# A second and third copy of the values in HBM, and attention units in mirrored order, on one Trainium2 core

## The chip, the cores and the metric

The kernel runs on one NeuronCore of a Trainium2 chip. Its engines run their own instruction queues and meet at semaphores: PE (TensorE, matrix products; the trace shows its weight loads apart as PEld), DVE (VectorE), ACT (ScalarE), POOL (GpSimd) and SP (SyncE, which here only issues DMAs). The metric is the device time of one execution in microseconds (us). A change of this kernel's time is told from no change at about 0.5%, some 14 us.

## The reference

One layer of a hybrid decoder, for a prompt of 2048 tokens and 64 sample tokens. The part that the change touches is the prompt's attention: 8 heads of 64 elements, and for each head three patterns of window and dilation, whose results are merged by their softmax denominators. Cut to that:

```
PATTERNS = ((128, 1), (512, 4), (2048, 16))          # window, dilation; n = window // dilation = 128

def dilated_prompt(q, k, v, window, dil):            # query t reads keys t - j*dil, j = 0..128
    qb, kb, vb = to_blocks(q), to_blocks(k), to_blocks(v)   # residue mod dil, blocks of 128
    kk, vv = with_prev(kb), with_prev(vb)                   # a block and the one before it
    s = jnp.einsum('brhcie,brhcje->brhcij', qb, kk) * (E ** -0.5)
    s = jnp.where(mask, s, NEG)                             # band, and no block before the first
    lse = jax.nn.logsumexp(s, axis=-1)
    p = jnp.exp(s - lse[..., None])
    return jnp.einsum('brhcij,brhcje->brhcie', p, vv), lse  # back in token order

def combine_patterns(results):
    w = jax.nn.softmax(lses, axis=0)
    return jnp.sum(w[..., None] * outs, axis=0)
```

Before it stand the projections of q, k, v and of a gated linear attention; behind it the output projection and a convolutional feed-forward network. Everything is float32; the large products are made of two fp32r parts each (high and low).

## The kernel before

**Stages.** By the trace, the projections of the linear attention run from 0 to about 480 us; the projections of q, k and v (`sweep_a`, one call per chunk of 512 tokens, in the order 3, 0, 1, 2), woven with the sample tokens' attention, from 480 to 780 us; the prompt's attention (`attention`) from 780 to 1090 us; the output projection and the feed-forward network from 1090 us to the end.

**Values.** `sweep_a` makes the values in tiles `vs` of 128 tokens by 256 elements (4 heads), 8 tiles per chunk. DVE copies each out of PSUM (L63), and one DMA of 128 KB stores it in the output `o_vp` (L453): on SP's queue for the chunks 3, 0 and 1, on POOL's for chunk 2. Rows of a chunk are ordered by residue modulo 16.

**Attention.** Loops run over 4 pairs of heads, 3 patterns and 4 groups of 4 blocks. A group is 2 units in patterns 0 and 1 and one unit in pattern 2, so a pair has 20 units. A unit (`AtUnit`) has three steps:

```
qk_  L1809  PE: scores of 2 or 4 blocks x 2 heads -> pas (3 PSUM buffers, a unit takes 2)
     L1814  DVE: add the mask, reduce to aml, -> ass      L1818  ACT: exp on ass, sums to aml
t    L1835  PE: up to 8 transposes of ass -> pat (2 PSUM buffers)
     L61/L63  ACT or DVE: copy pat -> apt, the copies dealt ACT ACT ACT DVE DVE in turn
pv   L1852  PE: 12 or 16 products of apt and the values av -> pao; after a group DVE copies pao -> aop
```

In the trace `pas`, `ass`, `pat`, `apt`, `pao` and `aop` are these tiles, `aml` the row extremes and sums, `c_ident` the identity. The products into `pao` use half of PE's columns (`128*64` in the trace); all others use `128*128`.

**Order.** Step i of the loop runs qk of unit i, t of unit i-2 and pv of unit i-3 (`skew=(2, 3)`; `fifo` and `drain`). In attention PE's order is the order of the code, by `AtUnit.line`; POOL's is too, by `Layer.line`. On ACT, DVE and SP a scheduler decides, by its own simulated costs. One step of the loop also advances the merge of the pair before (`pend`, `at_merge`): three POOL products with weights `awb`, which went through HBM as `d_awd`, and the gathers of the next queries, `aqg` (L1126), which POOL makes too.

**Loads.** `at_loadv` loads the values of a group into a tile `av` of 256 KB with four DMAs of 64 KB in pieces of 512 bytes (L1086, L1088, L1090 for the patterns 0, 1, 2), two groups ahead, on SP (the first two tiles on POOL). `at_load` (L1074) loads queries and keys of the next pair in pieces of 2 KB and more. Every DMA that SP and ACT issue takes one of 8 slots in turn and waits until the one 8 before it has landed.

Of the kernel before, what the change touches and what calls it, by code (L numbers as in the profile page):

```python
# [36 lines left out]
class Layer:  # L37
# [367 lines left out]
    def sweep_a(self, c):  # L405
        nc, a = self.nc, self.a
        xs = self.xnext
        u = 0
        for m in range(8):
            pr, isk = m // 2, m % 2  # L410
            wt = self.wget()
            for s0, n in self.subs(c):
                ps = self.psum.tile([128, 512], F32, name=self.n("pq"), tag="g1", bufs=3)
                self.gemm([(ps[:, :n], s0, n)], wt, xs, KT)
                npr = min(n, 512 - s0)
                if s0 == 0:
                    hi = self.st.tile([128, 512], F32R, name=self.n("qh"), tag="qh", bufs=2)
                    lo = self.st.tile([128, 512], F32R, name=self.n("ql"), tag="ql", bufs=2)
                src = ps[:, :npr]
                if isk:  # L420
                    self.split(hi[:, :npr], lo[:, :npr], src, "v")
                    nc.sync.dma_start(a["kh%d" % pr][c, :, s0:s0 + npr], hi[:, :npr].bitcast(F32))
                    nc.sync.dma_start(a["kl%d" % pr][c, :, s0:s0 + npr], lo[:, :npr].bitcast(F32))
                else:
                    rr = slice(s0 // 32, (s0 + npr) // 32)
                    hv, lv = (t.rearrange("p (i r) -> p r i", r=16)[:, rr, :] for t in (hi, lo))
                    sv = src.rearrange("p (r i) -> p r i", i=32)
                    nc.scalar.activation(hv, sv, AF.Copy, scale=-0.125)
                    nc.vector.scalar_tensor_tensor(lv, sv, -0.125, hv.bitcast(F32), op0=ALU.mult, op1=ALU.subtract)
                if isk:  # L430
                    kf = self.st.tile([128, 512], F32, name=self.n("kf"), tag="kf", bufs=2)
                    self.evac(kf[:, :n], ps[:, :n], "a")
                    nc.sync.dma_start(a["o_kp"][c, pr, :, s0:s0 + npr], kf[:, :npr])
                    if npr < n:
                        nc.sync.dma_start(a["o_ks"][pr], kf[:, npr:n])
                        nc.gpsimd.tensor_copy(self.ks[:, pr, :], kf[:, npr:n])
                elif npr < n:
                    qd = self.qbd[:, pr]
                    nc.vector.tensor_copy(qd[0:64, :, 0:8], ps[0:64, npr:n].rearrange("p (b t) -> p b t", b=8))
                    nc.vector.tensor_copy(qd[64:128, :, 8:16], ps[64:128, npr:n].rearrange("p (b t) -> p b t", b=8))  # L440
            if not isk:
                nc.sync.dma_start(a["qh%d" % pr][c], hi.bitcast(F32))
                nc.sync.dma_start(a["ql%d" % pr][c], lo.bitcast(F32))
            yield "q", m
        for nn in range(2):
            wv = [self.wget(), self.wget()]
            for t0, m in self.vblocks(c):
                ps = self.psum.tile([128, 512], F32, name=self.n("pv"), tag="g1", bufs=3)
                self.vgemm(ps, xs, t0, m, wv)
                vs = self.st.tile([128, 256], F32, name=self.n("vs"), tag="vs", bufs=self.AB["vsb"])  # L450
                self.evac(vs[:m], ps[:m, :256], "v")
                if m == 128:
                    (nc.gpsimd if c == 2 else nc.sync).dma_start(a["o_vp"][c * 512 + t0:c * 512 + t0 + 128, nn * 256:nn * 256 + 256], vs)  # L453
                else:
                    nc.sync.dma_start(a["o_vs"][:, nn * 256:nn * 256 + 256], vs[:64])
                yield "v", u
                u += 1
# [525 lines left out]
    def attention(self):  # L983
        with ExitStack() as ctx:
            self.aq[1] = self.pool(ctx, "at1")
            p = self.ap = self.pool(ctx, "at")
            self.app = self.pool(ctx, "atp", bass.MemoryType.PSUM)
            self.ev = 0
            pend = None
            fifo = []  # L990
            sk = self.AB["skew"]

            def drain(n):
                nonlocal pend
                if len(fifo) > sk[0]:
                    fifo[-1 - sk[0]].t()
                while len(fifo) > n:
                    un = fifo.pop(0)
                    un.t()
                    un.pv()  # L1000
                    if un.last:
                        for _ in pend or ():
                            pass
                        pend = self.at_merge(un.pr, un.ML, un.OP)

            if self.AB['man']:
                eng = mybir.EngineType
# [18 lines left out]
            for pr in range(4):  # L1026
                if pr == 3:
                    self.rctx.close()
                    pre = self.wo_pre()
                qk = self.qk0  # L1030
                nxt = self.at_load(pr + 1) if pr < 3 else iter(())
                ML, OP = [], []
                for pat in range(3):
                    base = 16 * (3 * pr + pat)
                    ml = p.tile([128, 16, 4], F32, name=self.n("aml"), tag=f"aml{pat}", bufs=2)
                    op = p.tile([128, 4, 512], F32, name=self.n("aop"), tag="aop", bufs=self.AB["op"])
                    ML.append(ml)
                    OP.append(op)
                    for g in range(4):
                        if base // 4 + g + 2 < 48:  # L1040
                            self.at_loadv(base // 4 + g + 2)
                        for _ in rest:
                            pass
                        po = [None]
                        nu = 1 if pat == 2 else 2
                        for u in range(nu):
                            fifo.append(AtUnit(self, pr, pat, g, u, nu, qk, base, ML, OP, po))
                            fifo[-1].qk_()
                            drain(sk[1])
                            if pat:  # L1050
                                next(pre, None)
                        if pend is not None:
                            next(pend, None)
                        if 5 <= 4 * pat + g < 11:
                            self.qk0 = next(nxt, self.qk0)
            for _ in pre:
                pass
            drain(0)
            for _ in pend:
                pass  # L1060
# [17 lines left out]
    def at_loadv(self, i):  # L1078
        nc, e = self.nc, self.nc.gpsimd if i < 2 else self.nc.sync
        pr, pat, n = i // 12, i // 4 % 3, i % 4  # L1080
        es = slice(128 * pr, 128 * pr + 128)
        vo = self.a["o_vp"]
        t = self.aq[1].tile([128, 4, 128], F32, name=self.n("av"), tag="av", bufs=self.AB["v"])
        for j in range(4):
            if pat == 0:
                e.dma_start(t[:, j, :], vo.rearrange("(c r b i) e -> c b r i e", c=4, r=16, b=4)[n, j, :, :, es])  # L1086
            elif pat == 1:
                e.dma_start(t[:, j, :], vo.rearrange("(c s r i) e -> r c s i e", c=4, s=4, r=4)[n, j, :, :, es])  # L1088
            else:
                e.dma_start(t[32 * j:32 * j + 32],  # L1090
                                  vo.rearrange("(c r i) e -> c i r e", c=4, r=16)[j, :, 4 * n:4 * n + 4, es])
        self.vq += [t[:, j] for j in range(4)]

    def at_operands(self, qk, h, pat, g, blk):
# [820 lines left out]
def pack_inputs(inp):  # L1915
# [14 lines left out]
    def vt(cols):  # L1930
# [28 lines left out]
    "o_ks": (4, 128, 64), "o_vs": (64, 512), "o_gs": (2, 128, 8, 128), "o_cs": (128, NF, 8, 2),  # L1959
}  # L1960
SCRATCH = {**{"%s%d" % (t, i): (4, 128, 512) for t in ("qh", "ql", "kh", "kl") for i in range(4)}, "awd": (3, 96, 128),
           "wbs": (12, 2, 128, 1024), "wst": (NF // 2, 2, 4, 128, 2, 512), "xst": (4, 14, 2, 128, 2 * H),
           "mixa": (128, 4, S), "mixb": (128, 4, T), "x1": (128, KT, T), "rs1": (128, T), "rs2": (128, T)}

# [15 lines left out]
def build(nc, arrays, stages="saf", ext_scratch=()):  # L1980
# [5 lines left out]
    with tile.TileContext(nc, **TCK) as tc:  # L1986
        with tc.tile_pool(name="scratch", bufs=1, space=bass.MemoryType.DRAM) as dp:
            for n, s in SCRATCH.items():
                if n in ext_scratch:
# [15 lines left out]
```

## Time and profile before

| | us |
|---|---|
| median of 3 runs | 2805.86 (2796.65 to 2811.69) |
| the profiled execution | 2799.56 |
| its span, first to last instruction | 2797.8 |
| projections of q, k, v: 480 to 780 | 300 |
| prompt attention: 780 to 1090 | 310 |
| the rest behind it: 1090 to 2798 | 1708 |
| PE busy over the span | 2685.3 (96%) |
| DVE, ACT, POOL busy over the span | 1844.2, 1268.5, 595.0 |

The profiled execution is 6.3 us below the median. A row of the timeline gives the start in us, the duration in us, the engine, the line, the operation, output and inputs, and the number of instructions; in brackets stands the idle time before it and what ended it. The chain of waits gives start, duration and what the end of the program hung on. In the tables by stretch the columns are PE, PEld, DVE, ACT and POOL busy (with instruction counts), PE's granted clock, the DMA engines' busy share and GB/s.

### The profile page before, as it was taken

How to read it: one execution, taken by the hardware profiler on the slowest of the kernel's cores; microseconds unless marked ns; L12 is line 12 of the kernel's file. 1: busy time of each engine (PE TensorE's matmuls, PEld its weight loads, DVE VectorE, ACT ScalarE, POOL GpSimd, SP SyncE). 2: the span in 40 equal slices, each digit the busy share in tenths (PEclk: the TensorE clock that was granted, in tenths of full speed). 3: DMA queues.
4: the chain of work that ended last, by engine and by line, in shares of the span. 5: the costliest groups of instructions: out<-in, count | busy, mean ns of one | idle time of the engine just before them, and what ended most of it. 6: DMA issues, size and time to landing. Idle time of an engine off the chain costs nothing.

```text
span 2797.8 us, 58627 instructions
## 1 busy us (share of the span) xinstructions
PE 2685.3 (96%) x22255; PEld 2532.2 (91%) x22255; DVE 1844.2 (66%) x4580; ACT 1268.5 (45%) x2959; POOL 595.0 (21%) x741
## 2 busy tenths in 40 slices
PE   7999999999989998998999998999999999999997
PEld 6788899878778787998999998999999999999997
DVE  7666655444347677466999888666577765666666
ACT  6535433333258676343654444434244333443332
POOL 3424243333333576012100011000020000200001
PEclk9999999999999999998999999999999999999998
DMA  8745536799798865367588678886698875976654
GB/s 300 260 169 178 179 117 210 260 327 373 261 217 172 188 165 148 105 217 259 177 299 302 224 277 293 284 294 226 209 333 281 299 236 199 330 254 212 222 190 144
DMA packets 283593, 656.82 MB, mean 235 GB/s; under 512 B 31840, under 2 KB 81632, under 8 KB 281264
## 3 DMA queue, kind: packets, MB, share of 16 engines
q1 hardware_dynamic: 253008, 574.66, 61.5%
q0 software_dynamic: 13216, 46.56, 5.0%
q10 hardware_dynamic: 17088, 31.86, 3.1%
q8 instruction: 175, 2.87, 0.4%
q14 instruction: 106, 0.87, 0.1%
HBM read 509.02 MB, written 143.94 MB: 233 GB/s over the span
## 4 chain that ended last, share of the span: by engine, by line
PE 76%; DMA 9%; DVE 7%; POOL 3%; ACT 2%; issue 2%; SPq 1%; ACTq 0%; DVEq 0%; POOLq 0%
PE pfd L90 17%; PE pv L396 9%; PE pfe L1581 8%; PE pfa L1581 8%; PE pfd L1581 8%; PE pq L90 7%; PE pbo L1427 5%; PE pfb L1581 4%; PE pas L1809 2%; PE pao L1852 1%; DMA ws<-d_wst 1%; PE pat L1835 1%; DMA raw<-in_xp 1%; DVE ws L71 1%; POOL aop L1225 1%
## 5 line engine op out<-in xcount | busy, mean ns | idle before, releaser
L68 ACT ACTIVATE ws<-wr 128x512 fp32r<-128x512 f32 (+1 forms) x482 | 293.1, 616 | 434.6 <-PE pfe L1581 138.4
L90 PE MATMUL pfd<-hh,ws 128*128 128x264 f32 x2816 | 477.3, 286 | 8.0 <-ACT ws L68 4.0
L90 PEld LDWEIGHTS pfd<-hh,ws 128*128 128x128 f32 x2816 | 401.7, 189 | 10.9 <-ACT ws L68 5.3
L71 DVE TENSOR_TENSOR ws<-wr,ws 128x512 fp32r<-128x512 f32 (+1 forms) x482 | 321.0, 672 | 134.7 <-ACT ws L68 131.8
L90 PE MATMUL pfd<-hl,ws 128*128 128x264 f32 x1408 | 304.7, 286 | 1.3 <-DVE hl L71 1.3
L1581 PE MATMUL pfa<-xh,ws 128*128 128x264 f32 x1496 | 293.0, 287 | 6.6 <-ACT ws L68 3.3
L1581 PE MATMUL pfe<-xh,ws 128*128 128x264 f32 x1496 | 290.6, 287 | 0.8 <-DMA ws<-d_wst 0.6
L1581 PE MATMUL pfd<-xh,ws 128*128 128x264 f32 x1408 | 289.0, 285 | 0.8 <-DMA ws<-d_wst 0.6
L1581 PEld LDWEIGHTS pfa<-xh,ws 128*128 128x128 f32 x1496 | 237.5, 190 | 8.6 <-ACT ws L68 5.0
L1581 PEld LDWEIGHTS pfe<-xh,ws 128*128 128x128 f32 x1496 | 238.2, 191 | 1.2 <-DMA ws<-d_wst 1.2
L396 PE MATMUL pv<-wh,xh 128*128 128x256 f32 (+1 forms) x816 | 234.8, 288 | 1.0 <-DVE th L693 1.0
L1581 PEld LDWEIGHTS pfd<-xh,ws 128*128 128x128 f32 x1408 | 231.8, 189 | 1.2 <-DVE ws L71 0.8
L396 PE MATMUL pv<-wl,xh 128*128 128x256 f32 (+1 forms) x816 | 232.3, 285 | 0.0
L396 PE MATMUL pv<-wh,xl 128*128 128x256 f32 (+1 forms) x816 | 231.6, 284 | 0.0
L90 PEld LDWEIGHTS pfd<-hl,ws 128*128 128x128 f32 x1408 | 226.9, 189 | 1.7 <-DVE hl L71 1.7
L1530 POOL DMA_DIRECT2D xl<-d_xst x52 | 28.6, 550 | 886.3 <-PE pfe L1581 856.9
L1818 ACT ACTIVATE ass<-ass,aml 128x256 f32<-128x256 f32 (+1 forms) x384 | 173.6, 455 | 89.3 <-DVE aml L1814 88.3
L1581 PE MATMUL pfd<-xl,ws 128*128 128x264 f32 x704 | 201.2, 286 | 0.0
L90 PE MATMUL pq<-xh,wh 128*128 128x512 f32 (+2 forms) x480 | 174.6, 371 | 10.6 <-ACT xh L234 8.2
L1581 PE MATMUL pfa<-xl,ws 128*128 128x264 f32 x616 | 176.8, 287 | 1.1 <-DMA xl<-d_xst 1.1
L1609 DVE TENSOR_TENSOR acc<-acc,pfd 128x264 f32<-128x264 f32 x304 | 116.9, 427 | 91.3 <-PE pfd L90 91.0
L1581 PE MATMUL pfe<-xl,ws 128*128 128x264 f32 x616 | 176.3, 286 | 0.0
(338 smaller groups left out, 6680.8 us busy)
## 6 DMA issues: line engine op xcount, KB each, us to landing
ws<-d_wst SPq DMA_DIRECT2D x248, 512.0 KB
wr<-in_wu SPq DMA_DIRECT2D x114, 512.0 KB
d_wst<-ws SPq DMA_DIRECT2D x88, 512.0 KB
wr<-in_wd SPq DMA_DIRECT2D x160, 256.0 KB
wr<-in_wt SPq DMA_DIRECT2D x60, 512.0 KB
wh<-d_wbs SPq DMA_DIRECT2D x35, 512.0 KB
wl<-d_wbs SPq DMA_DIRECT2D x35, 512.0 KB
skp<-in_ckt SPq DMA_DIRECT2D x16, 1024.0 KB
```

The source lines that it names most:

```text
L68: h = nc.scalar.activation(hi, src, AF.Copy)
L71: return h, (nc.gpsimd if lo_eng == "p" else nc.vector).tensor_tensor(lo, src, hi.bitcast(F32), op=ALU.subtract)
L90: mm = nc.tensor.matmul(o, ww[:, k, :], xx[:, s0:s0 + n], start=(k == order[0] and i == 0), stop=(k == order[-1] and i == 2))
L396: mm = nc.tensor.matmul(ps[:m, :256], x[:, t0:t0 + m], w[:, k % 4, :], start=(k == 0 and i == 0), stop=(k == KT - 1 and i == 2))
L1225: line(nc.gpsimd.tensor_tensor(OP[i][:, :, sl], OP[i][:, :, sl], W[:, i], op=ALU.mult))
L1427: self.lastmm = nc.tensor.matmul(o, ww[:, k, :], xx[:, s0:s0 + n], start=k == self.WORD[0] and i == 0, stop=k == self.WORD[-1] and i == 2)
L1530: self.nc.gpsimd.dma_start(t.bitcast(F32), xo[i, z])
L1581: self.lastmm = nc.tensor.matmul(bank[:, :H], w[:, ww, k, :], xx, start=new and k == 0 and j == 0, stop=k == 3 and j == 2, skip_group_chec ...
L1609: nc.vector.tensor_tensor(acc[m][:, s0:s0 + n], acc[m][:, s0:s0 + n], pz, op=ALU.add)
L1809: self.line(nc.tensor.matmul(ps[:, sc:sc + nk], lq, rk[z], start=(z == 0), stop=(z == 1)))
L1818: ex = nc.scalar.activation(ssb[:, sc:sc + nk], ssb[:, sc:sc + nk], AF.Exp, bias=self.ml[:, idx, h:h + 1], scale=-1.0, accum_out=self.ml[: ...
L1835: self.line(nc.tensor.transpose(ptp[:, len(tl), :], ssb[:, sc + 128 * j:sc + 128 * j + 128], L.ident))
```

## The change

It has three parts.

1. **Two more copies of the values.** Scratch tensors `v1` and `v2` of (4 pairs, 4 groups, 128, 512) hold the values in the order in which the patterns 1 and 2 read them. Behind the store of each `vs` tile stand four more stores of 64 KB, each of 128 pieces of 512 bytes. For the chunks 3, 0 and 1 all go to SP (96 more); for chunk 2 the first goes to POOL (8) and the other three to ACT (24), since `q` is bound anew in the loop.
2. **One load per tile.** `at_loadv` loads a tile of the patterns 1 and 2 with one DMA of 256 KB, 128 pieces of 2 KB, in place of four.
3. **Mirrored order.** Odd steps run qk, t, pv; even steps run pv, t, qk. The distances (2 and 3 units) stay.

```diff
                 if m == 128:
-                    (nc.gpsimd if c == 2 else nc.sync).dma_start(a["o_vp"][c * 512 + t0:..., nn * 256:...], vs)
+                    q = nc.gpsimd if c == 2 else nc.sync
+                    q.dma_start(a["o_vp"][c * 512 + t0:c * 512 + t0 + 128, nn * 256:nn * 256 + 256], vs)
+                    for z in range(2):
+                        for nm, q, rs, base in (("v1", q, 65536, 128 * t0 + 128 * c),
+                                                ("v2", nc.scalar if c == 2 else q, 128, 512 * t0 + 16384 * c)):
+                            v = a[nm][2 * nn + z]
+                            q.dma_start(bass.AP(tensor=v.tensor, offset=v.offset + base, ap=[[rs, 4], [512, 32], [1, 128]]),
+                                        vs[:, 128 * z:128 * z + 128])
...
+            def turn(first):
                 nonlocal pend
+                un = fifo.pop(0) if len(fifo) > sk[1] else None
+                pv = lambda: un and value(un)
+                tr = fifo[-1 - sk[0]].t if len(fifo) > sk[0] else lambda: None
+                for f in (tr, pv) if first else (pv, tr):
+                    f()
...
-                            fifo[-1].qk_()
-                            drain(sk[1])
+                            ups += 1
+                            if ups % 2:
+                                fifo[-1].qk_()
+                                turn(1)
+                            else:
+                                turn(0)
+                                fifo[-1].qk_()
...
+        if pat:
+            e.dma_start(t.rearrange("p j e -> p (j e)"), self.a["v%d" % pat][pr, n])
+        for j in range(0 if pat else 4):
+            e.dma_start(t[:, j, :], vo.rearrange("(c r b i) e -> c b r i e", c=4, r=16, b=4)[n, j, :, :, es])
```

(`value` is the old body: t, pv, and the start of a merge after a pair's last unit.) The lines of the changed file lie 18 further on in `AtUnit`: qk is L1827, reduce L1832, exp L1836, t L1853, pv L1870.

**ACT, first pair, pattern 0.** The names' numbers count the tiles; `ass` rows are exps, `apt` rows copies of transposes. Before:

```order
L1818 ACTIVATE ass_9492,aml_9386<-ass_9492,aml_9386 128x256 x2
L1818 ACTIVATE ass_9497,aml_9386<-ass_9497,aml_9386 128x256
L61 COPY apt_9507<-pat_9502 128x512
L1818 ACTIVATE ass_9497,aml_9386<-ass_9497,aml_9386 128x256
L1818 ACTIVATE ass_9542,aml_9386<-ass_9542,aml_9386 128x256 x2
L1818 ACTIVATE ass_9547,aml_9386<-ass_9547,aml_9386 128x256
L61 COPY apt_9564<-pat_9559 128x512
```

After, on the same engine at the same place:

```order
L1836 ACTIVATE ass_9643,aml_9516<-ass_9643,aml_9516 128x256 x2
L1836 ACTIVATE ass_9648,aml_9516<-ass_9648,aml_9516 128x256 x2
L1836 ACTIVATE ass_9669,aml_9516<-ass_9669,aml_9516 128x256 x2
L61 COPY apt_9691<-pat_9686 128x512
L1836 ACTIVATE ass_9674,aml_9516<-ass_9674,aml_9516 128x256 x2
L61 COPY apt_9716<-pat_9711 128x512
```

A copy stood behind three exps; now the copy `apt_9691` stands behind six, the four of one unit (9643, 9648) and the first two of the next (9669).

**DVE, the same place.** `ass` rows are reduces of scores; each stands there twice, with the read of its sum behind it (left out here). Before:

```order
L1814 ISA ass_9492,aml_9386<-pas_9482,atab_9104 128x256
L1814 ISA ass_9497,aml_9386<-pas_9487,atab_9104 128x256
L63 COPY apt_9514<-pat_9509 128x512
L1814 ISA ass_9542,aml_9386<-pas_9532,atab_9104 128x256
L1814 ISA ass_9547,aml_9386<-pas_9537,atab_9104 128x256
L63 COPY apt_9557<-pat_9552 128x512
```

After:

```order
L1832 ISA ass_9643,aml_9516<-pas_9633,atab_9206 128x256
L1832 ISA ass_9648,aml_9516<-pas_9638,atab_9206 128x256
L1832 ISA ass_9669,aml_9516<-pas_9659,atab_9206 128x256
L1832 ISA ass_9674,aml_9516<-pas_9664,atab_9206 128x256
L63 COPY apt_9684<-pat_9679 128x512
L63 COPY aop_9517<-pao_9612 128x4x128
```

A copy stood behind the four reduces of one unit; `apt_9684` stands behind the eight of two.

**PE, the same place.** Products that only repeat are left out (a pv has eight, each tile of scores four). Before:

```order
L1835 MATMUL pat_9502<-c_ident,ass_9435 128x128 x4
L1835 MATMUL pat_9509<-c_ident,ass_9440 128x128 x4
L1852 MATMUL pao_9516<-apt_9474,av_9349 64x128
L1809 MATMUL pas_9532<-akh_9147,aqs_9116 128x256
L1809 MATMUL pas_9537<-akh_9246,aqs_9209 128x256
L1835 MATMUL pat_9552<-c_ident,ass_9460 128x128 x4
L1835 MATMUL pat_9559<-c_ident,ass_9465 128x128 x4
L1852 MATMUL pao_9516<-apt_9507,av_9349 64x128
L1852 MATMUL pao_9516<-apt_9514,av_9349 64x128
```

After, from the first of two adjacent steps qk:

```order
L1827 MATMUL pas_9633<-akh_9253,aqs_9218 128x256
L1827 MATMUL pas_9659<-akh_9253,aqs_9218 128x256
L1853 MATMUL pat_9679<-c_ident,ass_9590 128x128 x4
L1853 MATMUL pat_9686<-c_ident,ass_9595 128x128 x4
L1870 MATMUL pao_9612<-apt_9624,av_9479 64x128
L1870 MATMUL pao_9702<-apt_9684,av_9479 64x128
L1870 MATMUL pao_9702<-apt_9691,av_9479 64x128
L1853 MATMUL pat_9711<-c_ident,ass_9643 128x128 x4
L1853 MATMUL pat_9718<-c_ident,ass_9648 128x128 x4
L1827 MATMUL pas_9725<-akh_9253,aqs_9218 128x256
```

Before, a pv, a qk and a t stood between a unit's transposes (`pat_9502`, `pat_9509`) and the products that read their copies (`apt_9507`, `apt_9514`); now, in every second unit, one pv (`pao_9612`) stands between `pat_9679`, `pat_9686` and the products that read `apt_9684`, `apt_9691`.

On SP the loads of the patterns 1 and 2 are 32 issues where they were 128.

More of the change, by code (lines that the diff above doesn't have):

```diff
@@ L452, in sweep_a @@
                 if m == 128:
-                    (nc.gpsimd if c == 2 else nc.sync).dma_start(a["o_vp"][c * 512 + t0:c * 512 + t0 + 128, nn * 256:nn * 256 + 256], vs)
+                    q = nc.gpsimd if c == 2 else nc.sync
[6 more added lines that the diff above has]
+                                        vs[:, 128 * z:128 * z + 128])
                 else:
@@ L991, in attention, with value @@
             sk = self.AB["skew"]
+            ups = 0
+            def value(un):
+                nonlocal pend
+                un.t()
+                un.pv()
+                if un.last:
+                    for _ in pend or ():
+                        pass
+                    pend = self.at_merge(un.pr, un.ML, un.OP)
             def drain(n):
+                while len(fifo) > n:
+                    value(fifo.pop(0))
+            def turn(first):
                 nonlocal pend
[L995 to L1004, printed above, removed]
+                un = fifo.pop(0) if len(fifo) > sk[1] else None
[3 more added lines that the diff above has]
+                    f()
             if self.AB['man']:
@@ L1083, in at_loadv @@
         t = self.aq[1].tile([128, 4, 128], F32, name=self.n("av"), tag="av", bufs=self.AB["v"])
[L1084 to L1091, printed above, removed]
+        if pat:
+            e.dma_start(t.rearrange("p j e -> p (j e)"), self.a["v%d" % pat][pr, n])
+        for j in range(0 if pat else 4):
+            e.dma_start(t[:, j, :], vo.rearrange("(c r b i) e -> c b r i e", c=4, r=16, b=4)[n, j, :, :, es])
         self.vq += [t[:, j] for j in range(4)]
@@ L1961 @@
 SCRATCH = {**{"%s%d" % (t, i): (4, 128, 512) for t in ("qh", "ql", "kh", "kl") for i in range(4)}, "awd": (3, 96, 128),
+           "v1": (4, 4, 128, 512), "v2": (4, 4, 128, 512),
            "wbs": (12, 2, 128, 1024), "wst": (NF // 2, 2, 4, 128, 2, 512), "xst": (4, 14, 2, 128, 2 * H),
```

## The prediction

> **What bounds the kernel now.** First the shares on the page, then a table by stretch (columns: length, then PE, PEld, DVE, ACT and POOL busy, PE's granted clock, the DMA engines' share, GB/s).
>
> ```profile
> PE 2685.3 (96%) x22255; PEld 2532.2 (91%) x22255; DVE 1844.2 (66%) x4580; ACT 1268.5 (45%) x2959; POOL 595.0 (21%) x741
> ...
> 480.00:780.00 300.00, 299.18 (x2560) 245.53 (x2559) 121.62 (x256) 94.39 (x124) 114.76 (x62) 1.00 0.83 300
> 780.00:800.00 20.00, 11.82 (x75) 10.55 (x74) 7.76 (x38) 10.31 (x39) 7.08 (x13) 0.83 1.05 251
> 780.00:1090.00 310.00, 277.57 (x2652) 244.26 (x2652) 211.02 (x961) 226.88 (x874) 174.17 (x186) 0.94 0.76 175
> 1090.00:2798.00 1708.00, 1653.75 (x13381) 1642.72 (x13379) 1213.43 (x2541) 717.96 (x1352) 127.76 (x268) 0.98 0.70 243
> ```
>
> PE is the bound. The projections leave it no gap (299.18 of 300 us), so there the change can only cost. The stretch behind 1090 us is not touched. All gain has to come from the attention, where PE idles 32 of 310 us; its first 20 us have the DMA engines full. Within the attention I read the chain of waits:
>
> ```profile
> 807.21 1.15 PE pas L1809 x8
> 808.35 0.87 PE pat L1835 x8
> 809.23 1.02 PE pao L1852 x16
> 810.25 1.14 PE pas L1809 x8
> ...
> 843.85 1.93 PE pas L1809 x16
> 845.78 0.90 PE pat L1835 x8
> 846.68 0.81 PE pao L1852 x12
> 847.49 1.94 PE pas L1809 x16
> ```
>
> In the first pair nothing but PE is on the chain: 3.04 us per unit in the patterns 0 and 1, 3.64 to 3.85 in pattern 2 (the x12 rows miss four of 16 records). In the later pairs the chain leaves PE:
>
> ```profile
> 954.51 8.01 DMA d_awd<-awt
> ...
> 963.33 9.66 DMA awb<-d_awd
> ...
> 1002.11 1.00 POOL aqg L1126
> ...
> 1003.15 0.88 PE pas L1809 x6
> ```
>
> ```profile
> L1195 POOL DMA_DIRECT2D d_awd<-awt x3: 527/528/539, 877.5 to 1031.7; - x3
> ```
>
> From the weights' store at 954.51 to the last gather that PE waits for, at 1003.15, are 48.6 us on DMA and POOL. Then come 28.5 us of PE until the next store at 1031.7. So in the third pair (954.51 to 1031.7) only the last 28.5 of 77 us hang on PE.
>
> **Part 3, the order.** What it saves: a product into `pao` uses another shape of the array than its neighbours, and entering and leaving it costs. Weight loads around one pv:
>
> ```profile
> 832.61 0.91 PEld L1835 LDWEIGHTS pat<-c_ident,ass 128*128 128x128 f32 x8
> 833.69 0.63 PEld L1852 LDWEIGHTS pao<-apt,av 128*64 128x64 f32 x12 [0.17 <-issue]
> 834.49 0.19 PEld L1809 LDWEIGHTS pas<-akh,aqg 128*128 128x128 f32 x1 [0.17 <-issue]
> ...
> 835.42 0.68 PEld L1835 LDWEIGHTS pat<-c_ident,ass 128*128 128x128 f32 x6
> ```
>
> There is 0.17 us of idle on either side. Eight loads of scores take 835.42 - 834.49 = 0.93 us, but in the chain 1.15 behind a pv: 0.22 lost. Four more products make a pv 0.21 longer (0.81 to 1.02), so 16 cost 0.84 and 0.18 is lost. A visit costs 0.40 us. With two pv side by side 40 of 80 visits go: at most 40 x 0.40 = 16 us, and only where PE sets the pace. [...]
>
> What it costs: in the order of the changed kernel every second unit has only one pv (1.02 us) between its transposes and the pv that reads their copies. What DVE and ACT do first is in the order shown: DVE all eight reduces of two units, ACT mostly five or six of their eight exps. Durations of these:
>
> ```profile
> 832.54 0.42 DVE L1814 CUSTOM_DVE_ANT_0 ass<-pas,atab 128x256 f32<-128x256 f32 x1
> ...
> 833.92 0.69 DVE L63 COPY apt<-pat 128x512 f32<-128x512 f32 x1
> ...
> 835.37 0.29 DVE L1814 CUSTOM_DVE_ANT_0 ass<-pas,atab 128x128 f32<-128x128 f32 x1 [0.77 <-PE pas L1809]
> ```
>
> ```profile
> 789.62 0.51 ACT L1818 ACTIVATE ass<-ass,aml 128x256 f32<-128x256 f32 x1
> ...
> 793.08 0.46 ACT L61 COPY apt<-pat 128x384 f32<-128x384 f32 x1
> ...
> 833.00 0.51 ACT L1818 ACTIVATE ass<-ass,aml 128x256 f32<-128x256 f32 x1 [0.39 <-DVE aml L1814]
> ...
> 845.72 0.39 ACT L1818 ACTIVATE ass<-ass,aml 128x128 f32<-128x128 f32 x1
> ...
> 847.26 0.56 ACT L61 COPY apt<-pat 128x512 f32<-128x512 f32 x1
> ```
>
> Four reduces fill 832.54 to 833.92, 0.345 each. The first starts 0.88 after the first weight load of its scores (835.37 - 834.49). The exp starts 0.46 after its reduce (833.00 - 832.54). Seven exps of 256 fill 789.62 to 793.08, 0.494 each; four of 128 fill 845.72 to 847.26, 0.385 each. A copy takes 0.69 on DVE, 0.56 on ACT.
>
> Let T be the first weight load of the two adjacent qk. PE comes to the second pv at T + 2 x 0.93 + 0.87 + 1.02 = T + 3.75. DVE has its copy at 0.88 + 8 x 0.345 + 0.69 = T + 4.33, a second one at 5.02. ACT has it at 0.88 + 0.46 + 6 x 0.494 + 0.56 = T + 4.86, after five exps 4.37. PE so waits 0.6 to 1.3 us. Behind the start of that pv come 0.84 of it, 0.22 and 0.87 of the even step's transposes: two units end at T + 6.3 to T + 6.95 against 6.08 before; without a wait it would be 5.68. I take 6.6, the middle, since ACT has three copies in five: +0.52 for two units. That PE also lacks a fourth `pas` buffer for two adjacent qk is hidden under this wait. In pattern 2 copies stand behind 10 to 16 exps of 128: ACT has them at 0.88 + 0.46 + 0.56 + 3.85 to 6.16 = 5.75 to 8.06, PE comes at 5.6 (3.7 + 0.90 + 1.02). The wait is 0.15 to 2.5, and 0.40 is saved: -0.25 to +2.1, of which I take 1.3, nearer to the upper end because the copies stand more often behind the sixteen.
>
> A pair has 8 cycles of two units in the patterns 0 and 1 and 2 in pattern 2: 8 x 0.52 + 2 x 1.3 = +6.8 us where PE sets the pace.
>
> **Part 2, the loads.** The waits for `av` in the second pair go:
>
> ```profile
> 897.99 0.44 PE L1852 MATMUL pao<-apt,av 128*64 128x128 f32 x4 [2.37 <-DMA av<-out_o_vp]
> ...
> 911.57 0.66 PE L1852 MATMUL pao<-apt,av 128*64 128x128 f32 x8 [3.91 <-DMA av<-out_o_vp]
> ...
> 912.96 0.70 PE L1852 MATMUL pao<-apt,av 128*64 128x128 f32 x4 [0.73 <-DMA av<-out_o_vp]
> ```
>
> They come to 7.0 us, with four issues each on SP's queue where one will stand. But POOL's gather is right behind:
>
> ```profile
> 923.96 2.11 POOL L1126 CAST aqg<-aqs 128x512 fp32r<-128x512 f32 x2
> ```
>
> ```profile
> 927.45 1.94 PE pas L1809 x16
> ```
>
> It ends at 926.07, and PE's scores of that group start at 927.45: only 1.4 us of the 7.0 show, unless POOL's chain gets shorter too. Its two transfers (8.01 and 9.66 us) share the DMA engines with fewer small pieces; I take 1 us for each of three pairs, between 0 and 3.
>
> **Part 1, the stores.** 96 more on SP, 8 on POOL, 24 on ACT's queue.
>
> ```profile
> L453 SPq DMA_DIRECT2D out_o_vp<-vs x24: 332/338/743, 487.4 to 696.9; - x24
> L453 POOL DMA_DIRECT2D out_o_vp<-vs x8: 539/544/731, 758.9 to 786.1; - x8
> ```
>
> ```profile
> SPq L453 <- DVE vs L63: 33.0, 18, 7.0
> ```
>
> 96 x 0.34 = 33 us of SP's queue, as much as SP waits before such stores now (33.0 us); so the queue is about full while they go. Behind them stand the next chunk's loads of weights, and PE has no gap to hide a late one. The bytes fit: 128 x 64 KB = 8.4 MB at 300 GB/s for a share of 0.83 are 23 us of the engines' 300, of which 51 are free. Bounds: nothing (all hidden) and 8 us (two late weights of 4 us). I take 2, nearer to nothing, because the loads run ahead. POOL's 8 x 0.54 us stand before the first values' loads there. The 24 on ACT are for the last chunk, in the stretch whose DMA share is 1.05, before the first keys and values:
>
> ```profile
> 801.12 0.55 PE L1809 MATMUL pas<-akh,aqs 128*128 128x256 f32 x1 [4.02 <-DMA akh<-d_kh]
> 803.02 0.55 PE L1809 MATMUL pas<-akl,aqs 128*128 128x256 f32 x1 [1.35 <-DMA av<-out_o_vp]
> ```
>
> The 32 stores of 64 KB of chunk 2 are 2.1 MB; at 251 GB/s 8 us if all of them came ahead of those loads, 0 if none. I take 4.
>
> **The sum**, on the profiled execution (2799.56 us): first pair +7 (all on PE); second pair +1 (+6.8 and -7.0 on PE, but not below POOL's -1.4); third pair +3.6 - 1 (28.5 us on PE with two cycles of pattern 2 and two others); last pair +2 (the same part of it, less the transfers' 1 and what its merge hides); start +4; stores +2. That is +18.6, so 2818; the median of the runs is 6.3 above the profiled execution, so 2824.
>
> **The rivals.**
> - *Faster: the copies are in time.* If ACT and DVE get to the copies by T + 3.75, each two units save 0.40: first pair 10 x 0.40 = 4, second 1.4 + 1 and some, third 4 x 0.40 + 1, last 2. With the start and the stores hidden that is -11 to -16, so 2790 to 2795; if POOL's chain gave way too, up to -23 (16 + 7), 2783. The point that decides is whether the copy is behind more than three reduces or exps (0.88 + 0.46 + 4 x 0.494 + 0.56 = 3.88). The 0.17 us of idle speak for it; the order of DVE and ACT against it. Chance 0.15. [...]
> - *Nothing to see: POOL and the transfers set the pace.* If the start and the stores cost nothing and the waits fall on what POOL makes PE wait for anyway, the first pair's +7 and the shorter transfers' -3 remain: 2806 to 2812. For it speaks the chain of 48.6 us; against it the first pair, which is PE alone. Chance 0.23.
> - *Slower by the stores.* SP's queue is full, weights come late at two changes of chunk and the first keys too: 8 + 8 in place of 2 + 4, with the order's waits 2834, and up to 2850 if each of four late weights cost 4 us. Against it speaks the DMA share of 0.83. Chance 0.10.
>
> **The numbers.** The forecast has 0.52, its own range 2812 to 2838. Less than 0.5% (14 us) cannot be told from no change. Slower by more than that: two thirds of the forecast and the third rival, 0.46. Within 0.5%: the rest of the forecast, nearly all of the second rival, 0.39. Faster: the first rival, 0.15. The range of 2794 to 2846 leaves out the lower half of the first and the end of the third.
>
> **What would show it.** Right: on PE, pv rows waiting 0.6 to 1.3 us for `apt`, once in two units; two units 6.6 us apart in the first pair; visits to the half-width shape halved; no wait for `av` in the second pair; SP's loads of values one issue per tile in the patterns 1 and 2. The step on the order is wrong if two units take 5.7 us, that on the stores if 480 to 780 us grows by more than 8. The prediction as a whole fails if the third and last pair's POOL chain shortens by more than the few us taken here, or if more of a pair hangs on PE.

## The result, and the profile after

The changed kernel takes 2865.18 us (median; 2862.32 to 2873.33) against 2808.78 for the kernel before in the same runs: a ratio of 1.0225, 95% interval 1.0203 to 1.0247. It is slower, as forecast, but by 56 us of these medians, or 63 by the ratio, where 18 were forecast, and 2865 lies above the range.

Three stretches of the profiled execution (span 2871.5 us), with the columns of the table by stretch in the prediction: the projections, the start of attention (first scores at 815 us, 781 before), the rest of attention.

```profile
480.00:780.00 300.00, 278.69 (x2273) 221.39 (x2273) 114.95 (x241) 90.41 (x119) 100.56 (x47) 0.96 0.83 299
780.00:860.00 80.00, 49.70 (x415) 44.34 (x414) 16.69 (x62) 14.95 (x46) 30.67 (x37) 0.79 0.79 210
860.00:1170.00 310.00, 270.18 (x2594) 235.43 (x2593) 211.03 (x932) 221.34 (x844) 171.20 (x180) 0.97 0.62 153
```

The first row is the surprise: PE had no gap there before (299.18 of 300), now it lacks 21 us and its clock falls to 0.96, while the DMA share (0.83) and the rate (299 GB/s against 300) have not moved. PE's timeline names what came late: the sample tokens' cached values (`svp`), the next chunk's input (through ACT's `xh`), and at the start of attention the keys (`akl`, `akh`).

```profile
630.69 1.94 PE L539 MATMUL pso<-svp,spt 128*32 128x128 f32 x32 [4.33 <-DMA svp<-in_cv]
639.70 1.22 PE L90 MATMUL pq<-xh,wh 128*128 128x512 f32 x2 [7.08 <-ACT xh L68]
...
736.89 1.08 PE L539 MATMUL pso<-svp,spt 128*32 128x128 f32 x16 [4.82 <-DMA svp<-in_cv]
...
819.63 0.45 PE L1827 MATMUL pas<-akl,aqs 128*128 128x128 f32 x1 [4.79 <-DMA akl<-d_kl]
832.45 0.45 PE L1827 MATMUL pas<-akh,aqs 128*128 128x128 f32 x1 [11.84 <-DMA akh<-d_kh]
840.76 0.44 PE L1827 MATMUL pas<-akl,aqs 128*128 128x128 f32 x1 [7.86 <-DMA akl<-d_kl]
```

SP's timeline shows what stands before them. The input's loads (`raw`) of 633.73 us come behind some 20 us of nothing but value stores and one load:

```profile
612.63 7.20 SPq L459 DMA_DIRECT2D d_v<-vs  x4
...
624.66 3.12 SPq L459 DMA_DIRECT2D d_v<-vs  x4
628.21 2.81 SPq L454 DMA_DIRECT2D out_o_vp<-vs  x1
631.08 2.54 SPq L459 DMA_DIRECT2D d_v<-vs  x4
633.73 0.74 SPq L227 DMA_DIRECT2D raw<-in_xp  x1
```

In the attention the waits for values are gone, and two others are new: for the copies `apt` and for `aml` (columns: us in total, times, longest). Before, and after:

```profile
PEld pao L1852 <- DMA av<-out_o_vp: 11.8, 6, 4.1
```

```profile
PEld pao L1870 <- ACT apt L61: 25.2, 32, 2.4
...
PEld pas L1827 <- DVE aml L1832: 11.7, 7, 4.9
PEld pao L1870 <- issue: 10.1, 38, 3.5
PEld pao L1870 <- DVE apt L63: 6.4, 18, 0.6
```

The first and the last row are the products that wait for the copies `apt`, as forecast. The second row was not forecast: scores wait for DVE's reduces at the change from one pair of heads to the next. PE there, and DVE at the same time:

```profile
1062.34 1.09 PE L1870 MATMUL pao<-apt,av 128*64 128x128 f32 x16 [2.17 <-ACT apt L61]
...
1079.25 0.58 PE L1827 MATMUL pas<-akh,aqs 128*128 128x256 f32 x1 [4.11 <-DVE aml L1832]
```

```profile
1070.20 2.03 DVE L63 COPY aop<-pao 128x512 f32<-128x512 f32 x2 [1.92 <-POOL aop L1228]
...
1073.91 1.98 DVE L1177 TENSOR_TENSOR amm<-aw,aml 128x32 f32<-128x32 f32 x1
...
1078.43 0.41 DVE L1832 CUSTOM_DVE_ANT_0 ass<-pas,atab 128x256 f32<-128x256 f32 x1
```

From 1070.20 to 1078.43 DVE does copies and the merge of the pair that has just ended, and no reduce of scores. Two adjacent steps qk need four `pas` buffers, there are three, and so PE stops at the fourth. Before, the gap at such a place (1019.63 us) was 0.51 us.

### The profile page after: what moved, and what is told of

Same layout as the page of the kernel before. It is cut to its first block, busy times and chain, and to the rows that moved or that the text cites. A ratio compares the mean times of both kernels' runs of the same rounds, so it can differ in the third digit from the quotient of the medians.

```text
span 2871.5 us, 58697 instructions
## 1 busy us (share of the span) xinstructions
PE 2699.0 (94%) x22255; PEld 2535.4 (88%) x22255; DVE 1846.0 (64%) x4580; ACT 1269.7 (44%) x2959; POOL 600.4 (21%) x749
## 5 line engine op out<-in xcount | busy, mean ns | idle before, releaser
L1836 ACT ACTIVATE ass<-ass,aml 128x256 f32<-128x256 f32 (+1 forms) x384 | 172.4, 451 | 87.5 <-DVE aml L1832 87.5
L90 PE MATMUL pq<-xl,wh 128*128 128x512 f32 (+2 forms) x480 | 174.9, 366 | 0.1
```

The lines of the kernel that those rows point to most:

```text
L90: mm = nc.tensor.matmul(o, ww[:, k, :], xx[:, s0:s0 + n], start=(k == order[0] and i == 0), stop=(k == order[-1] and i == 2))
L1836: ex = nc.scalar.activation(ssb[:, sc:sc + nk], ssb[:, sc:sc + nk], AF.Exp, bias=self.ml[:, idx, h:h + 1], scale=-1.0, accum_out=self.ml[: ...
```

## The experiments

"Old order" is the order of the kernel before. Ratios are against the kernel before on the same chip. "First scores", "seventh unit" (of the first pair) and "last unit" are starts in the profiled execution, in us. Some kernels do the same work on other numbers, so their output is not the layer's: e6, e7 and e11 load the tiles of the patterns 1 and 2 from a part of `o_vp` that lies in one piece, and e12 and e14 permute the values in the copies. "Spread" is said here of stores and loads that walk the same addresses with a dimension of 32 outermost in place of 4.

| kernel | ratio (95% interval) | first scores | seventh unit | last unit |
|---|---|---|---|---|
| before | 1 | 781 | 810 | 1074 |
| after | 1.0225 (1.0203 to 1.0247) | 815 | 863 | 1145 |
| e1 stores and loads, old order | 1.0171 (1.0152 to 1.0191) | 811 | 855 | 1112 |
| e2 order only | 1.0056 (1.0035 to 1.0077) | 781 | 810 | 1092 |
| e3 after, ACT's stores on POOL | 1.0249 (1.0232 to 1.0265) | 807 | 847 | 1144 |
| e4 after, SP's stores on POOL | 1.0188 (1.0162 to 1.0215) | 794 | 839 | 1120 |
| e5 e1 with half the stores, 1 KB pieces | 1.0097 (1.0073 to 1.0120) | 798 | 836 | 1094 |
| e6 e1 without chunk 2's stores | 1.0080 (1.0059 to 1.0101) | 810 | 841 | 1099 |
| e7 loads only | 0.9969 (0.9955 to 0.9982) | 779 | 808 | 1064 |
| e8 pv in pairs, with cover | 0.9999 (0.9986 to 1.0013) | 781 | 809 | 1074 |
| e9 e5 with SP's stores on POOL | 1.0059 (1.0038 to 1.0080) | 787 | 825 | 1086 |
| e10 e9 for pattern 1 alone | 1.0012 (0.9996 to 1.0029) | 783 | 817 | 1077 |
| e11 e8 and e7 together | 0.9963 (0.9949 to 0.9978) | 781 | 808 | 1066 |
| e12 e1 with the stores spread | 1.0060 (1.0040 to 1.0081) | 795 | 835 | 1091 |
| e13 before, pattern 1's loads spread | 0.9972 (0.9959 to 0.9986) | 778 | 807 | 1066 |
| e14 e5 with the stores spread | 1.0006 (0.9992 to 1.0020) | 782 | 813 | 1071 |

**e1 and e2: the parts.** e1 is the changed kernel with the old loop of `attention`; e2 is the kernel before with the new loop.

> The extra stores and the one-DMA loads, with the units in the old order. Theory 1 (the stores' places in the queues cost most): about +40 to +45 us against before: +30 between 480 and 780 us (SP's queue), +20 at the start of attention (ACT's queue), and -5 for the values' waits that go. Theory 2 (the new order costs most): at most +10 us, and the stretch from 480 to 780 us grows only because something in attention moves back into it. Theory 3 (the two only hurt together): below +20.

> The mirrored order alone: no extra stores, values loaded by four DMAs as before. Theory 1: +10 to +16 us, nothing of it before 780 us, nearly all in the last pair of heads, with waits of products into pao for apt of 0.3 to 0.5 us in patterns 0 and 1 and 1.3 to 2.2 us in pattern 2, and one wait of scores for DVE's merge of 4 us per pair. Theory 2: +40 us or more. My prediction's term for it alone: +12.

0.0171 and 0.0056 add up to 0.0227, against 0.0225 for the whole: no interaction is seen beyond the intervals of some 6 us. Stores and loads cost 48 us (0.0171 x 2801), the order 16. That is theory 1's split, and theory 2 falls; why the stores cost so much, places in queues or something else, these two do not tell. In e2 two units of pattern 0 take 6.8 to 6.9 us by the weight loads of each first pv:

```profile
812.04 0.85 PEld L1867 LDWEIGHTS pao<-apt,av 128*64 128x64 f32 x16 [0.17 <-issue]
...
818.83 0.85 PEld L1867 LDWEIGHTS pao<-apt,av 128*64 128x64 f32 x16 [0.17 <-issue]
...
825.76 0.85 PEld L1867 LDWEIGHTS pao<-apt,av 128*64 128x64 f32 x16 [0.17 <-issue]
826.89 0.19 PEld L1867 LDWEIGHTS pao<-apt,av 128*64 128x64 f32 x2 [0.28 <-ACT apt L61]
827.76 0.63 PEld L1867 LDWEIGHTS pao<-apt,av 128*64 128x64 f32 x10 [0.67 <-ACT apt L61]
```

The last two rows are a second pv that waits twice for copies.

**e3 and e4: another queue.**

```diff
-  ("v2", nc.scalar if c == 2 else q, ...)        # e3: chunk 2's extra stores all on POOL
+  ("v2", q, ...)
...
+  q = nc.gpsimd if z == 0 or c != 2 else nc.scalar   # e4: chunks 3, 0, 1 on POOL
```

> The changed kernel, but the 24 extra stores of the last chunk that stood on ACT's queue go to POOL's queue, beside the 8 that are there. Theory 1: the first exp no longer comes some 30 us behind the first scores; 15 to 20 us less than the changed kernel, so about +38 against before. Rival (the bytes of these stores, 2.1 MB in a stretch where the DMA engines are full, set the start): no more than 5 us less than the changed kernel.

> The changed kernel, but the 96 extra stores of the chunks 3, 0 and 1 go to POOL's queue and none of them to SP's; the last chunk as in the changed kernel. Theory 1 (SP's queue: loads stand behind stores in it): the stretch from 480 to 780 us loses its 30 us, so 20 to 30 us less than the changed kernel, unless POOL, which also splits the weights, gets late by 96 x 0.74 = 71 us of issues (then about the same loss in another place, PE waiting for wl). Rival (the bytes: 8.4 MB more in 300 us): no change, within 5 us of the changed kernel.

e3 refutes theory 1 for the start: at the end nothing is gained. The first scores come 8 us earlier and the seventh unit 16, but now the first values' loads stand behind 32 stores on POOL, and a second wait for values follows behind the seventh unit, so that 1 us is left at the last unit:

```profile
835.17 1.55 PE L1870 MATMUL pao<-apt,av 128*64 128x128 f32 x12 [12.39 <-DMA av<-out_o_vp]
...
861.33 1.55 PE L1870 MATMUL pao<-apt,av 128*64 128x128 f32 x12 [10.00 <-DMA av<-out_o_vp]
```

e4 brings the first scores from 815 to 794, 21 of 34 us, and by the ratio some 10 us, below the 20 to 30 expected. So taking the stores off SP helps, but 13 us stay. It is not the queue alone that changed: on POOL's queue the trace has these stores as packets of 4096 bytes, on SP's as packets of 512, and e4, e3 and e9 do not tell the two apart. No run here moves a store between SP's queue and ACT's; e3, from ACT's queue to POOL's, bought nothing.

**e5 and e6: how many, and which.** e5 stores two pairs of heads at once (128 KB in pieces of 1 KB); e6 leaves out the stores of chunk 2.

```diff
-  v = a[nm][2 * nn + z]; ... ap=[[rs, 4], [512, 32], [1, 128]]), vs[:, 128 * z:128 * z + 128])
+  v = a[nm][nn];         ... ap=[[2 * rs, 4], [1024, 32], [1, 256]]), vs)          # e5
...
-  for z in range(2):
+  for z in range(2 if c != 2 else 0):                                                # e6
```

> Old order of units; extra stores and one-DMA loads as in the first experiment, but the scratch tensors hold two pairs of heads side by side, so two stores of 128 KB in pieces of 1 KB take the place of four of 64 KB in pieces of 512 bytes: the same 8.4 MB by 64 extra DMAs in place of 128. (The loads are then one DMA in pieces of 512 bytes.) Theory 1 (number of issues and slots in the queues): about half of the first experiment's +50, +20 to +28 us. Rival (bytes): +42 to +50.

> Old order of units; the extra stores of the chunks 3, 0 and 1 as they are, those of chunk 2 left out, and the loads of patterns 1 and 2 read 256 KB of the output o_vp in one DMA in place of the scratch tensors (other values, the same bytes and pieces). Theory 1: the start of attention costs nothing more, from the first scores to the seventh unit some 29 us as before and not 44; +28 to +34 us. Rival (the start is late only because the projections end late): +45 or more.

e5 costs 27 us in place of 48, as theory 1 said; but it changed the pieces too, so it did not tell why. e6 falls to 22, below the 28 to 34 expected, and from first scores to seventh unit it takes 31 us, near the 29 of the kernel before and not the 44 of e1: this stretch is long through chunk 2's stores, and not because the projections end late.

**e7, e8 and e11: what the other two parts are worth by themselves.**

```diff
+  if pat: e.dma_start(t.rearrange("p j e -> p (j e)"), vo[1024 + 128 * n:1152 + 128 * n])   # e7
...
   fifo[-1].qk_()
+  if ups % 2: drain(...)          # e8: two pv at once, four and three units behind
+  fifo[-3].t()
```

> The old kernel without any extra store; the loads of patterns 1 and 2 are one DMA of 256 KB from o_vp in pieces of 2 KB (other values, as many bytes). Theory 1: what part 2 is worth by itself, -5 to -8 us (first experiment: pairs of heads of 74, 75 and 63 us against 76, 78 and 65). Rival (POOL's gathers were right behind): -1 to -2 us, no difference.

> No extra stores, old loads. Two pv still stand side by side, so the visits to the half-width shape are halved, but a qk step and a pv stand between a unit's transposes and the pv that reads their copies: PE's order is qk, pv, pv, t, qk, t, with pv four units behind qk. Theory (halved visits are worth 0.40 us for two units once the copies are in time): 5.7 to 5.9 us for two units in the first pair, and -3 to -8 us in all. Rival (the visits cost nothing that another wait does not take): within 2 us of before. If the copies are late here too: +5 or more.

> The order of the eighth experiment (pv in pairs with a qk and a pv as cover) and the loads of the seventh (one DMA per tile, other values, no extra stores). Theory (the eighth gained on PE and lost it to waits for values, which are loaded as late as before while pv comes a unit later in pairs): -12 to -16 us against before, more than the -8.8 of the loads alone. Rival (POOL's chain of the merge is the floor under both): -7 to -10, as the loads alone.

The loads alone gain 0.31%, some 9 us (5 to 13), where 5 to 8 were expected. e8 gains nothing. Its rows show both halves of that. The visits cost up to what was read from the trace: 32 products run without the 0.17 us of idle, and in pattern 1 two units take 5.3 to 5.5 us:

```profile
822.72 1.73 PEld L1856 LDWEIGHTS pao<-apt,av 128*64 128x64 f32 x32
828.19 1.51 PEld L1856 LDWEIGHTS pao<-apt,av 128*64 128x64 f32 x28
833.46 1.51 PEld L1856 LDWEIGHTS pao<-apt,av 128*64 128x64 f32 x28
```

In the kernel before they take 5.66, so 0.2 to 0.4 us are saved where 0.40 had been read:

```profile
830.61 0.85 PEld L1852 LDWEIGHTS pao<-apt,av 128*64 128x64 f32 x16 [0.17 <-issue]
...
836.27 0.85 PEld L1852 LDWEIGHTS pao<-apt,av 128*64 128x64 f32 x16 [0.17 <-issue]
```

But what the first pair gains (2 us at its last units) is lost again in the later pairs. Part of that are longer waits for values (11.8 us in the kernel before) and for POOL's gathers (8.5 before), in e8:

```profile
PEld pao L1856 <- DMA av<-out_o_vp: 14.1, 3, 6.5
PEld pas L1813 <- POOL aqg L1130: 10.1, 6, 2.5
```

With the loads made early too, e11 is no faster than the loads alone (0.9963 against 0.9969), which is the time that the rival gave. Its cause is shown in part only: e11 starts the last pair of heads 3.4 us before e7 and takes 68.5 us for it where e7 takes 63.2; the chain of waits there runs over POOL from 1045.38 to 1058.00 us, but at other places over ACT's exps and DVE's copies, and no run takes one of these away.

**e9 and e10: cheaper stores.**

```diff
+  q = nc.gpsimd                                     # e9: on e5; chunk 2's v2 stays on ACT
-  for nm, q, rs, base in (("v1", ...), ("v2", ...)):
+  for nm, q, rs, base in (("v1", ...),):            # e10: on e9; pattern 2 loads as before
```

> The two stores of 128 KB of the fifth experiment, with those of the chunks 3, 0 and 1 on POOL's queue (48) and none of the extra ones on SP's; old order of units, loads as in the fifth. Theory 1 (SP's queue by the number of issues): the projections cost +3 to +6 us in place of some +17 to +20, the start +9 as there, the loads give 7 to 9 back: +5 to +10 us in all. Rival (bytes are the rest of the loss): +15 or more, and the DMA share near 1 between 600 and 680 us.

> As the ninth experiment, but only the copy that pattern 1 reads is stored (32 stores, all on POOL's queue), and pattern 2 loads as in the old kernel. Theory 1: projections +1 to +3 us, start +4, loads -4 to -7 (the waits for av stood mostly in pattern 1): -3 to +3 us, the same as before. Rival: +8 or more, if one more store per tile already makes loads late.

e9 came out above its 5 to 10 us, at 16, and with a DMA share of 1.02 between 600 and 680 us: both are the signs of the rival, that the bytes are the rest of the loss (e14 below, with as many bytes, speaks against it). The projections cost 6 us as expected, the start 9 as in e5, and the loads, now in pieces of 512 bytes, gave by that sum little back. In e10 one copy about pays for itself: 3 us by the ratio, between 1 less and 8 more.

**e12 to e14: the spread.** By then what made one store so dear was open. The extra stores have 4 outermost. e12 walks the same addresses with the 32 outermost, which also makes each store of `v2` one contiguous stretch; e14 does it to e5; e13 does it to the loads of pattern 1 in the kernel before, which have 4 outermost as well.

```diff
-  ap=[[rs, 4], [512, 32], [1, 128]]                                   # e1
+  ap=[[512, 32], [rs, 4], [1, 128]]                                   # e12
...
-  e.dma_start(t[:, j, :], vo.rearrange("(c s r i) e -> r c s i e", c=4, s=4, r=4)[n, j, :, :, es])
+  e.dma_start(t[32 * j:32 * j + 32], vo.rearrange("(c s r i) e -> r s i c e", c=4, s=4, r=4)[n, j, :, :, es])   # e13
```

> The first experiment with one thing changed: each extra store walks the same addresses of the scratch tensors with the dimension of 32 outermost in place of the one of 4 (the values in the tensors are permuted, so the output is not the reference's). Number of stores, bytes, pieces of 512 bytes, queue and order are the same. [...] Theory 1 (number of issues and their order in SP's queue): within 8 us of the first experiment, +40 to +50; only the stores of v2, which become plain ones, are issued in 0.34 us in place of 0.53.

> The old kernel with one thing changed: the four loads of a tile of pattern 1 are cut by 32 partitions each (32 x 4 x 128, as pattern 2 does it) in place of by 128 columns each (4 x 32 x 128); as many DMAs, bytes and pieces, no extra stores. [...] Theory 1 (the number of issues in SP's queue was what delayed the values): within 2 us of before.

> The fifth experiment (64 stores of 128 KB, old order) with the dimension of 32 outermost in place of 4 (values permuted in the scratch tensors). If the spread and the number of stores are two separate costs: +27 less the spread's part, +3 to +8 us, and the first scores by 790 us. If the spread is all and the number of stores costs nothing: as the twelfth, +14 to +18. If the number is all that was left: 0 or below, the loads' gain showing.

e12 costs 17 us (11 to 23) where e1 costs 48: just above the 15 of the author's estimate, far from the 40 to 50 of theory 1. With as many stores in the same places, 31 us are gone. The issue of one store is no shorter, by SP's rows (e1, then e12; min, median, max in ns); in total the 96 rows take 67 us and 58, since fewer of them are long:

```profile
L459 SPq DMA_DIRECT2D d_v<-vs x96: 508/528/2601, 485.4 to 730.5; - x96
```

```profile
L459 SPq DMA_DIRECT2D d_v<-vs x96: 320/559/1996, 484.1 to 718.7; - x96
```

For the extra stores of e1 the view has a time to landing only for the eight on POOL (KB each, median us):

```profile
d_v<-vs SPq DMA_DIRECT2D x96, 64.0 KB
...
d_v<-vs POOLq DMA_DIRECT2D x8, 64.0 KB, 5.9
```

For the others, how long a store is under way is read from the updates of its semaphore that the trace has from the DMA side: 5 for each of the 120 extra stores on SP and ACT in e1, 16 for each in e12 (and 16 for each of the 128 KB stores beside them, in both). From its issue to its last update a store on SP takes 4.4 us in e1 and 2.7 in e12 (medians of 96). And while one is under way, SP's queue never has more than 7 packets of 512 bytes in flight in e1, and up to 21 in e12. The traces do not name the engine of a packet, so what lies behind these counts is not shown.

The rate changed too, between 600 and 680 us, when most stores of a chunk go: before, e1, e12 and e14 in this order.

```profile
600.00:680.00 80.00, 80.00 (x667) 63.88 (x669) 35.55 (x66) 30.15 (x38) 32.06 (x15) 1.00 0.95 354
```

```profile
600.00:680.00 80.00, 67.54 (x527) 49.59 (x527) 31.15 (x58) 24.46 (x32) 28.24 (x13) 0.89 0.91 334
```

```profile
600.00:680.00 80.00, 71.63 (x540) 53.73 (x539) 35.05 (x59) 26.73 (x35) 28.56 (x14) 0.94 0.96 356
```

```profile
600.00:680.00 80.00, 79.48 (x651) 63.40 (x652) 36.80 (x66) 29.50 (x38) 31.04 (x15) 1.00 1.01 376
```

In e1 the engines move less than before (334 against 354 GB/s) although more is asked of them; with half the stores and these spread they move 376 and PE has 79.5 of its 80 us back. In e14 stores and loads together cost 2 us by the ratio (2 less to 6 more), just under the 3 to 8 expected for two costs and not to be told from zero, and the bytes are those of e1 and e12. So there are two costs that stand side by side, the order of the walk and the number of stores (with half the stores the pieces are twice as large, 1 KB, which no run takes apart from the number): 48 us with neither mended, 27 with half the stores, 17 with the spread, 2 with both.

e13 computes what the kernel before computes and is faster than both kernels, by 0.28% (0.14 to 0.41%), some 8 us. It changes neither the number of loads nor their bytes. Each of these loads has 16 updates of its semaphore from the DMA side, where those of the kernel before have 5. The issue takes 0.43 us in place of 0.56, the 64 rows together 27 us in place of 84, and the waits for values are nearly gone (e13's row for the loads of pattern 1, and its waits):

```profile
L1088 SPq DMA_DIRECT2D av<-out_o_vp x64: 311/426/1479, 796.0 to 1029.2; - x64
```

```profile
PEld pas L1810 <- POOL aqg L1127: 13.3, 12, 3.0
...
PEld pao L1853 <- DMA av<-out_o_vp: 2.2, 4, 1.7
```

Against that stand 528/564/6679 ns and 11.8 us of waits in the kernel before. So most of what one DMA per tile is worth (e7, 9 us) can be had with as many issues as before.

## Why the prediction was wrong

By the ratios, the 63 us are: stores of the chunks 3, 0 and 1, e6 less e7, 0.0111 or 31 us; stores of chunk 2, e1 less e6, 0.0091 or 26; the loads, e7, -9; the order, e2, 16. Each is uncertain by some 6 us or more. (The traces show 13 of chunk 2's 26 us between first scores and seventh unit; where the other 13 lie, single executions do not tell.)

- **The stores, put at +2 with an upper end of 8, cost 31.** This is the step that failed. The queue was read rightly ("the queue is about full while they go"), and then covered with "the loads run ahead". PE's rows show that they did not: 4.33 and 4.82 us of waiting for `svp`, 7.08 for the input behind `raw`, then the keys, while PE had no gap to hide them in. That the bytes fit (23 us of the engines' 300, with 51 free) was an average over 16 engines; what the stores cost follows the order in which they walk their addresses, by e12 (31 us less than e1), and how many they are, by e5 (21 less, with the pieces twice as large). The price of an issue was taken from the store that was there, 0.34 us; the new ones, with three dimensions, took 0.53.
- **The start, put at +4 of 0 to 8, cost 13 to 26.** The bound counted bytes again, 8 us at the most; 13 is the stretch up to the seventh unit, e1 against e6, and 26 the difference of their ratios.
- **The loads** were held back by "but POOL's gather is right behind", which allowed 1.4 us and the transfers' 3. They gave 9: in e7 the waits for values are nearly gone, and POOL's third store of weights goes at 1023.6 us in place of 1031.7.
- **The order** came out near in one step: two units at 6.3 to 6.95 us were worked out, 6.6 taken and 6.8 to 6.9 measured, and the waits for `apt` are where they were put. That its 16 us lie near the 12 that e2's expectation names as the prediction's term is luck: by pair, from its first scores to those of the next or to the last unit, e2 takes +5, -2.5, +2.4 and +13.4 us against the kernel before (single executions), where the sum has +7 for the first pair, +3.6 for the third and +2 for the last (in the second it sets the order's +6.8 against the loads). "last pair +2" took POOL to set the pace there. The chain of waits does run over POOL in the kernel before, but PE is close behind: that pair takes 65 us, PE's 16 x 3.04 + 4 x 3.85 are 64, and PE's weight loads wait for POOL's gathers 3.9 us in it. So this pair pays in e2 as PE does, 13 us, above the 6.8 worked out for a pair. That the lack of a fourth `pas` buffer is hidden held inside a pair and not at its end, where it costs 4.1 us at the change shown above.
- **The rivals.** "Slower by the stores" had the mechanism, a chance of 0.10 and an end of 2850, which the time passed. "The copies are in time" was tried as e8: the saving is there on PE in the first pair, and it does not reach the end.

## What to carry to other kernels

In this kernel a DMA that was added had three prices besides its bytes: its issue (0.53 us for a store of 64 KB on SP's queue), what stands behind it in its queue (PE waited 7.08 us for the input behind `raw`), and the order of its walk (e12's stores, with 32 outermost in place of 4, cost 31 us less than e1's); try that order before counting bytes over all engines. A queue that would be as full as it now waits has no cover, whatever the average says, and a bottleneck engine without gaps behind it pays at once, as PE did between 480 and 780 us (278.69 us busy of 300, 299.18 before). Saving on the bottleneck engine by pulling steps together takes away the cover that lay between them, and pays only as far as no other wait stands just behind (e2 lost 16 us, e8 gained nothing).

## What the hardware showed

- The same addresses walked with 4 or with 32 outermost: stores of 64 KB on SP's queue are under way 4.4 and 2.7 us, with 5 and 16 updates of the semaphore from the DMA side and at most 7 and 21 packets in flight, and the kernels take 2851 and 2823 us (1.0171 and 1.0060). The traces do not name the engine of a packet.
- Loads of 64 KB with 4 outermost take 0.56 us to issue on SP, with 32 outermost 0.43.
- Moving chunk 2's 24 extra stores from ACT's queue to POOL's saved nothing (1.0249 against 1.0225); on POOL's queue they went as packets of 4096 bytes in place of 512.
